# A fused decoder layer: sums for the up-projection made by adding DMAs inside the mixing layer

## The chip, the cores and the metric

The kernel runs on one core of a Trainium2 chip. The metric is the device time of one execution in microseconds (us); the kernel before takes 1341.85 us (median of three runs, 1340.24 to 1342.94).

Five engines work beside each other, each through its own list of instructions in order: PE (TensorE, matmuls), DVE (VectorE), ACT (ScalarE), POOL (GpSimd) and SP (SyncE, which here only issues transfers). DMAs are issued from SP, from ACT and from POOL; those of POOL can add to what lies at the destination instead of replacing it, and only they do so here. An instruction that waits holds up whatever stands behind it on its engine, and a DMA that waits holds up the later DMAs of the same issuing engine.

## The reference

One decoder layer in float32, on 1024 tokens of width 1024: a norm, one wide input projection, two attention mixers (differential and sliding-window), gates, an output matrix, a residual sum, a second norm, and a gated feed-forward part with a causal convolution. What this change touches begins at the output matrix:

```python
        merged = jax.nn.sigmoid(g_da) * (y_da @ w_br_da[l]) + jax.nn.sigmoid(g_sw) * (y_sw @ w_br_sw[l])
        x = x + merged @ w_mix_out[l]
        xn = rmsnorm(x, norm_ffn_w[l])
        x = x + conv_ffn(xn, w_up[l], conv_w[l], conv_b[l], w_down[l])
    return rmsnorm(x, norm_final_w)
```

`conv_ffn` multiplies by `w_up` (1024 x 5632), runs a convolution of width 3 along the tokens, multiplies one half by the silu of the other, and multiplies by `w_down` (2816 x 1024).

## The kernel before, in words

Everything is kept transposed: features on the 128 partitions, the 1024 tokens along the free axis, in two halves of 512 (`H2`). A feature block is called m or k.

**Two parts per operand.** Each float32 operand is split into a high part (a cast to float32r on ACT) and a low part (the difference, on DVE), and each product is three matmuls: high by high, high by low, low by high (`mm3`, `product`). A weight unit is therefore a load (SP), a cast on ACT (`wh`, line 142, or `sh`/`wh`, line 121) and a subtraction on DVE (`wl`, line 144, or `sl`/`wl`, line 123). The raw weights of all stages turn through three buffers called `raw` (`RAW = 3`), each free again when its subtraction is done.

**Seven products in place of eight.** The input projection, the output matrix ("mixing layer"), the up-projection ("hidden layer") and the down-projection each use a Strassen-Winograd scheme: a 2 x 2 block product by seven block products P1 to P7 (`STAGES`), whose operands include sums: S1 to S4 of weight blocks, T1 to T4 of activation blocks.

**Where sums are made before.** For the mixing layer and the down-projection the weight sums are made far ahead in DRAM by `sums_of` (line 85): copies issued by SP and adding DMAs issued by POOL, `md` for the mixing layer, four of its 32 steps behind each of the nine weight pairs of the input projection. For a pair of weight blocks of the input projection and of the up-projection they are made on POOL by `sum_pair` (four operations, lines 107 to 110), from two loads (`raw`, line 102, and `rv`, line 104); `split_pair` then splits A11/A12, S1/S2, S3/S4 and A22.

**The mixing layer** (`mix`, line 853) has seven stages of two halves each. This document calls these fourteen halves units 0 to 13: P1 is units 0 and 1, P2 units 2 and 3, P5 4 and 5, P6 6 and 7, P3 8 and 9, P7 10 and 11, P4 12 and 13. A unit takes one weight load of 512 KB and runs 24 matmuls (two feature blocks, four k, three matmuls each) into PSUM banks; behind each 12 of them DVE adds the bank to the residual tile `xm` (line 955, "eviction"). Four of the seven stages finish a quarter of the new x: P2 (blocks 0 to 3, first half of the tokens), P3 (0 to 3, second half), P7 (4 to 7, second half) and P4 (4 to 7, first half). `finish` (line 888) then stores it to DRAM (`x2d`, issued by ACT), squares it on ACT and adds the square to `rstd` on POOL (line 898). `onward` (line 900), at most one block later, makes the operands of the hidden layer from it: x times the norm weight, and the sums and splits B11, T1, B22, T3, T2, T4 and B21.

- For blocks 0 to 3, ACT multiplies `xm` by the norm weight in place (line 904), so it has to wait until the store of that same tile is done.
- The sums are DVE operations: `t` (line 908), `u` (line 913), `t + u` (line 914) and T4's `u` (line 919), four of each, 128 x 512.
- In P3, behind unit 9's weights, `sum_pair` loads the first up-projection pair into two of the three `raw` buffers and sums it on POOL. It is split only at the end of `mix` (`split_pair`, lines 121 and 123), so both buffers are held until then.

**The hidden layer** (`hidden`, line 993) runs 22 pairs of 84 matmuls each, pair 0 in the order P1, P5, P3, P7, P2, P6, P4 with the norm's column sums in between. After each pair DVE recombines the seven banks (`recombine`, line 469), POOL or DVE scales by `rstd`, ACT and DVE run the convolution (lines 1153 to 1156).

**What sets the order.** A scheduler orders each engine's list by priorities (`tc.high_priority` moves work forward) and by hand-written rules (`tc.issue_after` keeps work behind a named instruction). Tile pools free memory for later pools.

## Time and profile before

| what | value |
|---|---|
| median of three runs | 1341.85 us (1340.24 to 1342.94) |
| the profiled execution | 1340.74 us, span of the trace 1339.0 us |
| busy share of the span | PE 98%, PE weight loads 81%, DVE 81%, ACT 47%, POOL 38% |
| granted TensorE clock | 0.990 of full speed on average |
| packets' time on the DMA queues | SP's 40.8%, POOL's 8.5%, ACT's 3.6% of 16 engines' span |
| mixing layer in the trace | 587.7 to 690.7 us |
| hidden layer in the trace | 690.7 to 1118 us |

How to read the rows: in the table by stretches of time each row gives the start and end in us from the span's start, the length, then for each engine its busy us and in brackets its instructions, then the granted TensorE clock, the busy share of the 16 DMA engines and GB/s. In lists in order of time, the first column is the start in us and the second the busy us of the (merged) entry; a bracket at the end gives the idle time before it and what ended it. "SPq" and the like are instructions that only the engine's queue handles, such as issuing a DMA. Grouped rows give min/median/max in ns, then first and last start. A matmul row gives 0.39 us for one matmul, but they are pipelined: the distance from one start to the next is what counts.

### The profile page before, as it was taken

To read this page: it belongs to the slowest core of one execution; us is meant where nothing else is said; L and a number is where in the kernel's file an instruction comes from. 1 tells how busy PE (TensorE), PEld (TensorE's weight loads), DVE (VectorE), ACT (ScalarE), POOL (GpSimd) and SP (SyncE) were. 2 spreads that over 40 slices of the span, in tenths; PEclk is the share of its full clock that TensorE was granted. 3 is DMA by queue.
4 is the path that set the end of the run, shared out by engine and by line. 5 is a ranking of instruction groups with operands and counts; after the bars stand their busy time and mean duration, and the time that the engine had idled before them with its cause. 6 is when DMAs were issued, how large, how long until landed. Compare 5 with 4: busy or idle time off the path is not lost.

```text
span 1339.0 us, 17280 instructions
## 1 busy us (share of the span) xinstructions
PE 1306.0 (98%) x6162; PEld 1084.2 (81%) x6162; DVE 1087.8 (81%) x1518; ACT 634.4 (47%) x1002; POOL 510.3 (38%) x396
## 2 busy tenths in 40 slices
PE   9999999999999999998889999999999999999997
PEld 7888888888888878886668888888888887888886
DVE  8856685388898977656887999999999999896855
ACT  9432232376667774334554334343343335554543
POOL 0448662010101017742435666676667642000002
PEclk9999999999999999999989999999999999999999
DMA  7346665966554146567342434663636237953534
GB/s 290 134 178 160 227 214 149 281 169 177 157 135 150 64 160 187 165 215 201 110 142 91 181 127 134 168 202 105 202 122 160 80 103 249 331 183 119 162 96 146
DMA packets 81414, 221.71 MB, mean 166 GB/s; under 512 B 9008, under 2 KB 16816, under 8 KB 81072
## 3 DMA queue, kind: packets, MB, share of 16 engines
q1 hardware_dynamic: 61536, 183.37, 40.8%
q0 software_dynamic: 6912, 19.93, 8.5%
q10 hardware_dynamic: 12880, 17.31, 3.6%
q8 instruction: 48, 0.79, 0.2%
q14 instruction: 38, 0.31, 0.1%
HBM read 167.62 MB, written 80.22 MB: 185 GB/s over the span
## 4 chain that ended last, share of the span: by engine, by line
PE 76%; DVE 11%; issue 5%; DMA 3%; ACT 2%; POOL 2%; SPq 0%; POOLq 0%; DVEq 0%; ACTq 0%
PE t L990 29%; PE y L1209 9%; PE d L1209 7%; PE g L163 4%; PE g L164 4%; PE g L165 4%; PE m L953 3%; PE sc L649 3%; DVE c L1155 2%; DVE wl L123 2%; PE t L665 1%; DMA rv<-in_w_up 1%; PE sc L165 1%; PE sc L164 1%; PE sc L163 1%
## 5 line engine op out<-in xcount | busy, mean ns | idle before, releaser
L144 DVE TENSOR_TENSOR wl<-raw,wh 128x1024 fp32r<-128x1024 f32 (+2 forms) x91 | 111.6, 1229 | 47.2 <-ACT wh L142 37.5
L142 ACT CAST wh<-raw 128x1024 fp32r<-128x1024 f32 (+2 forms) x91 | 80.3, 885 | 85.8 <-PE y L1209 44.1
L1139 POOL TENSOR_TENSOR us<-us,rstd 128x1024 f32<-128x1024 f32 x42 | 94.9, 2307 | 47.6 <-DVE us L482 31.2
L1153 ACT ACTIVATE c<-us,vecs 128x1024 f32<-128x1024 f32 x44 | 54.8, 1247 | 116.0 <-POOL us L1139 110.5
L990 PE MATMUL t<-T,sh 128*128 128x512 f32 x352 | 109.2, 391 | 0.2 <-DVE u L477 0.2
L180 POOL TENSOR_TENSOR rs<-ms,mhalf 128x8 f32<-128x8 f32 (+2 forms) x9 | 14.2, 1580 | 238.8 <-DVE ms L178 232.6
L123 DVE TENSOR_TENSOR sl<-sf,sh 128x1024 fp32r<-128x1024 f32 x62 | 90.6, 1462 | 14.8 <-ACT sh L121 14.7
L121 ACT CAST sh<-sf 128x1024 fp32r<-128x1024 f32 x62 | 64.6, 1044 | 79.9 <-PE t L990 40.6
L107 POOL TENSOR_TENSOR sf<-rv 128x512 f32<-128x512 f32 x30 | 56.8, 1894 | 105.2 <-DMA rv<-in_w_up 52.9
L990 PE MATMUL t<-x,wh 128*128 128x512 f32 x248 | 82.2, 389 | 0.0
L953 PE MATMUL m<-x,wh 128*128 128x512 f32 x192 | 63.6, 418 | 15.1 <-ACT wh L142 15.1
L990 PEld LDWEIGHTS t<-T,sh 128*128 128x128 f32 x352 | 65.5, 188 | 15.0 <-DVE u L477 1.6
L163 PE MATMUL g<-xh,wh 128*128 128x512 f32 x176 | 70.9, 403 | 1.5 <-ACT g L578 1.5
L1156 DVE SCALAR_TENSOR_TENSOR c<-us,vecs,c 128x1024 f32<-128x1024 f32 x44 | 72.2, 1674 | 0.1
L164 PE MATMUL g<-x,wh 128*128 128x512 f32 x176 | 70.3, 400 | 0.0
L165 PE MATMUL g<-xh,wl 128*128 128x512 f32 x176 | 70.2, 399 | 0.0
L1155 DVE SCALAR_TENSOR_TENSOR c<-us,vecs,c 128x1024 f32<-128x1024 f32 x44 | 67.4, 1561 | 1.9 <-ACT c L1153 1.7
L990 PE MATMUL t<-T,sl 128*128 128x512 f32 x176 | 68.6, 390 | 0.0
L990 PE MATMUL t<-x,sh 128*128 128x512 f32 x212 | 68.2, 389 | 0.0
L109 POOL TENSOR_TENSOR sf<-raw,rv 128x512 f32<-128x512 f32 x30 | 54.0, 1798 | 35.5 <-DVE sl L123 35.5
L123 DVE TENSOR_TENSOR wl<-raw,wh 128x1024 fp32r<-128x1024 f32 (+1 forms) x32 | 65.9, 2059 | 0.1
L1209 PE MATMUL y<-h,wh 128*128 128x512 f32 (+1 forms) x224 | 65.2, 375 | 0.0
(335 smaller groups left out, 3944.0 us busy)
## 6 DMA issues: line engine op xcount, KB each, us to landing
u<-qd SPq DMA_DIRECT2D x72, 256.0 KB, 6.4
raw<-in_w_up SPq DMA_DIRECT2D x23, 512.0 KB, 4.8
raw<-in_w_in SPq DMA_DIRECT2D x22, 512.0 KB, 4.9
hd<-c SPq DMA_DIRECT2D x22, 512.0 KB, 2.6
sdP<-in_w_down POOLq DMA_DIRECT2D x16, 704.0 KB, 8.3
rv<-in_w_up SPq DMA_DIRECT2D x21, 512.0 KB, 3.6
hc<-hd SPq DMA_DIRECT2D x33, 256.0 KB, 5.5
gr<-gd SPq DMA_DIRECT2D x16, 512.0 KB, 4.6
```

The costliest lines, as they stand in the source:

```text
L123: low = nc.vector.tensor_tensor(lo, src, hi.bitcast(F32), ALU.subtract)
L142: self.hi = nc.scalar.copy(wh, raw)
L144: self.lo = (eng or nc.vector).tensor_tensor(wl, raw, wh.bitcast(F32), ALU.subtract)
L163: nc.tensor.matmul(ps, wh[:, kc + o, :], ah, start=first and n == 0, stop=False)
L164: nc.tensor.matmul(ps, wh[:, kc + o, :], al, start=False, stop=False)
L165: nc.tensor.matmul(ps, wl[:, kc + o, :], ah, start=False, stop=last and n == len(kcs) - 1)
L953: nc.tensor.matmul(ps, v[:, m % 2 * 4 + k, :], x, start=start and k == i == 0, stop=k == 3 and i == 2, skip_group_check=True)
L990: nc.tensor.matmul(ps, (ah, ah, al)[p][:, k, :], (bh, bl, bh)[p], start=first and n == p == 0, stop=last and p == 2 and n == len(ks) - 1, ...
L1139: i = (nc.vector if m % NF == 0 else nc.gpsimd).tensor_tensor(us[:, 2:], us[:, 2:], self.rstd, ALU.mult)
L1155: nc.vector.scalar_tensor_tensor(c, us[:, 1:T + 1], cw[1], c, ALU.mult, ALU.add)
L1156: nc.vector.scalar_tensor_tensor(c, us[:, 0:T], cw[0], c, ALU.mult, ALU.add)
L1209: nc.tensor.matmul(ps, v[:, k - k0, :], x, start=start and k == i == 0, stop=k == HK - 1 and i == 2, skip_group_check=True)
```

## The change: what it does

**Weight sums of the first two up-projection pairs** (`NPRE = 2`) are made in DRAM, in new tensors `ud`, by `sums_up`: for each of the two pairs four copies issued by SP and four adding DMAs issued by POOL, 256 KB each, in a chain (S1 and S3 from copies of weights, S2 from S1, S4 from S2). They follow the mixing layer's sums in one chained list, and the loop of the input projection now issues six steps behind each weight pair instead of four. As a DMA only adds, S2, S3 and S4 come out in forms whose signs are turned; activation operands take the signs over, and `recombine` adds or subtracts accordingly (`pre`), and gives its operands in the other order.

**Loads of these two pairs** go by `part_pair`: four parts, each one load through `raw`, one cast on ACT, one subtraction on DVE: A11/A12, S1/S2, S3/S4, and A22 (half the size). POOL's four operations per pair go away for both. In `mix`, parts 1 and 2 of pair 0 are asked for behind the weights of units 12 and 13, and parts 0 and 3 after the last unit. `sum_pair` in P3 goes away.

**Activation sums** are made by 16 adding DMAs, each 256 KB within SBUF, issued by POOL: `onward` and its 16 DVE sums go away. ACT makes a scaled copy (8 more ACT operations, for B22 and B21), and the work is put off by whole units: a function `later` files it under a unit number, and `run_due` issues it behind that unit's weight cast and subtraction. Scaling in place comes two units after the eviction, T1 is split one unit after its add; B22 is split one unit after the eviction, T3 two and T2 three; B21 one, T4 two. What falls due after unit 13 is issued at the end of `mix`.

**Order and memory.** `next_w` in `mix` stands under `tc.high_priority(60)`; the splits of the merged activations stand at the start of the next stage, behind its weights. The pool `sfp` of POOL's sums is opened only in `hidden`, after the `xm` tiles are given up.

```diff
@@ ahead
             if nk == "pair":
                 first, skip = eng or (False, 0)
-                self.wq.append(self.split_pair(*self.sum_pair(src, first), skip))
+                if len(src) == 3:
+                    w = {}
+                    for part in range(4):
+                        w.update(self.part_pair(src, part))
+                    self.wq.append(w)
+                else:
+                    self.wq.append(self.split_pair(*self.sum_pair(src, first), skip))
...
+    def sums_up(self):
+        nc, d = self.nc, self.ud
+        row = lambda j, r: self.w_up[j].rearrange("p k c -> p (k c)")[:, r * H2:(r + 1) * H2]
+        copy = lambda n, src: lambda j: nc.sync.dma_start(d[j][:, n], src(j))
+        add = lambda n, o, r: lambda j: nc.gpsimd.dma_start(d[j][:, n], row(j + o, r), accum_op=ALU.add)
+        for step in (copy(0, lambda j: row(j + NF, 0)), copy(2, lambda j: row(j + NF, 0)), add(0, NF, 1), add(2, 0, 0),
+                     copy(1, lambda j: d[j][:, 0]), add(1, 0, 0), copy(3, lambda j: d[j][:, 1]), add(3, 0, 1)):
+            for j in range(NPRE):
+                step(j)
+                yield
+
+    def part_pair(self, src, part):
+        nc = self.nc
+        raw = self.tl(self.wp, [P, 1 if part == 3 else 2, 4, P], "raw", bufs=RAW)
+        nc.sync.dma_start(raw.rearrange("p a k c -> p (a k) c"), (src[0], src[2][:, 0:2].rearrange("p a (k c) -> p (a k) c", k=4),
+                          src[2][:, 2:4].rearrange("p a (k c) -> p (a k) c", k=4), src[1][:, 4:8])[part])
+        n = (("A11", "A12"), ("S1", "S2"), ("S3", "S4"), ("A22",))[part]
+        pool, h, l = (self.uw, "sh", "sl") if part in (1, 2) else (self.wp, "wh", "wl")
+        hi = self.tl(pool, [P, len(n), 4, P], h, F32R)
+        self.hi = nc.scalar.copy(hi, raw)
+        lo = self.tl(pool, [P, len(n), 4, P], l, F32R)
+        self.lo = nc.vector.tensor_tensor(lo, raw, hi.bitcast(F32), ALU.subtract)
+        if part == 0:
+            self.front = self.hi.ins, self.lo.ins
+        return {name: (hi[:, i], lo[:, i]) for i, name in enumerate(n)}
@@ project
-            sums = self.sums_of(self.md, self.w_mix, H2)
+            sums = chain(self.sums_of(self.md, self.w_mix, H2), self.sums_up())
...
-                for _ in range(4):
+                for _ in range(6):
@@ recombine
-        tt(c11, ps["P2"], s1, ALU.add)
-        tt(u2, ps["P6"], s1, ALU.add)
-        tt(u3, ps["P7"], u2, ALU.add)
...
+        sub = lambda flag: ALU.subtract if flag else ALU.add
+        tt(c11, s1, ps["P2"], sub(o))
+        tt(u2, ps["P6"], s1, sub(pre))
+        tt(u3, u2, ps["P7"], sub(pre))
...
@@ mix
-        def onward(m, hf):
...
-                if hf == 0:
-                    self.B["B11", k] = parts(up["B11", k], x)
-                else:
-                    tt(t, x, col(k, 0), ALU.subtract)
-                    self.B["T1", k] = parts(up["T1", k], t)
-            elif hf:
-                self.B["B22", k] = parts(up["B22", k], x, wcol(m))
-                u = col(k, 1)
-                stt(u, x, wcol(m), u, ALU.mult, ALU.subtract)
-                tt(t, u, col(k, 0), ALU.add)
...
+        add = lambda x, y: nc.gpsimd.dma_start(x, y, accum_op=ALU.add)
+        later = lambda i, f: due.setdefault(i, []).append(f)
...
+            if m < 4 and hf == 0:
+                later(i + 2, lambda: (nc.scalar.mul(x, x, wcol(m)), put("B11", k, x)))
+            elif m < 4:
+                later(i + 2, lambda: (nc.scalar.mul(x, x, nw[:, m:m + 1]), add(col(k, 0), x)))
+                later(i + 3, lambda: put("T1", k, col(k, 0)))
             elif hf:
+                t = x22[k // 2][:, k % 2]
+                later(i + 1, lambda: (nc.scalar.mul(t, x, wcol(m)), put("B22", k, t), add(col(k, 1), t)))
+                later(i + 2, lambda: (add(col(k, 0), t), put("T3", k, col(k, 1))))
+                later(i + 3, lambda: put("T2", k, col(k, 0)))
             else:
+                t = col(m, 1)
+                later(i + 1, lambda: (nc.scalar.mul(t, x, nw[:, m:m + 1]), put("B21", k, t), add(col(k, 0), t)))
+                later(i + 2, lambda: put("T4", k, col(k, 0)))
...
+        def run_due(i):
+            with tc.issue_after(self.hi.ins), tc.issue_after(self.lo.ins):
+                for f in due.pop(i, ()):
+                    f()
...
                 for h in range(2):
-                    w = self.next_w()
+                    with tc.high_priority(60):
+                        w = self.next_w()
+                        if stage == "P4":
+                            self.uw = uw
+                            w0.update(self.part_pair(pair, 1 + h))
+                            self.uw = None
...
-                    if stage == "P3" and h:
-                        i = [e[1] for e in self.wsrc].index("pair")
-                        pair = self.sum_pair(self.wsrc.pop(i)[0], True)
+                    run_due(i)
...
-        with tc.high_priority(100):
-            return self.split_pair(*pair)
+        with tc.high_priority(60):
+            for part in (0, 3):
+                w0.update(self.part_pair(pair, part))
+        run_due(i)
+        run_due(i + 1)
+        run_due(i + 2)
...
+        return w0
```

More of the change, by code (lines that the diff above doesn't have):

```diff
@@ L2 @@
 from contextlib import ExitStack, nullcontext
+from itertools import chain
 import numpy as np
@@ L27 @@
 RAW = 3
+NPRE = 2
 HP, HPB, HR = 7, 13, 11
@@ L216, in run @@
             self.md = {n: self.dp.tile([4, P, H2], F32, name="md" + n) for n in ("P5", "P6", "P3", "P7")}
+            self.ud = [self.dp.tile([P, 4, H2], F32, name=f"ud{j}") for j in range(NPRE)]
             self.sd = {n: self.dp.tile([4, P, HK * P], F32, name="sd" + n) for n in ("P5", "P6", "P3", "P7")}
@@ L258, in plan @@
                 src.append((w, KC))
-        src += [((self.w_up[j], self.w_up[j + NF]), "pair") for j in range(NF)]
+        src += [((self.w_up[j], self.w_up[j + NF], *self.ud[j:j + 1]), "pair") for j in range(NF)]
         for name in STAGES:
@@ L863, in mix @@
         self.B = {}
[L864 to L865 removed]
+        self.tctx, sctx = ExitStack(), ExitStack()
         xmp = self.tctx.enter_context(tc.tile_pool(name="xmp", bufs=1, reuse_waits="tile"))
[L867 to L873 removed]
+        xm = {m: xmp.tile([P, T], F32, name=f"xm{m}") for m in range(KC)}
+        sqp = sctx.enter_context(tc.tile_pool(name="sqp", bufs=1, reuse_waits="tile"))
+        sqs = [sqp.tile([P, 2, H2], F32, name="sqs")]
+        x22 = [self.tl(self.cpl, [P, 2, H2], "c") for _ in range(2)]
+        nw = self.st.tile([P, KC], F32, name="nw")
+        nc.vector.tensor_scalar(nw, self.vecs[:, C_NF:C_NF + KC], -1.0, None, ALU.mult)
+        acc, nsq = self.rstd, []
         col = lambda m, hf: xm[m][:, hf * H2:(hf + 1) * H2]
         wcol = lambda m: self.vecs[:, C_NF + m:C_NF + m + 1]
+        due = {}
         def parts(t, src, scale=None):
@@ L886, in parts, with put, finish @@
             return hi, lo
-        def finish(m, hf):
-            x = col(m, hf)
+        def put(name, k, src, scale=None):
+            t = self.slot(k) if name == "T3" else self.slot(4 + k) if name == "B21" else up[name, k]
+            self.B[name, k] = parts(t, src, scale)
+        add = lambda x, y: nc.gpsimd.dma_start(x, y, accum_op=ALU.add)
+        later = lambda i, f: due.setdefault(i, []).append(f)
+        def finish(i, m, hf):
+            x, k = col(m, hf), m % 4
             nc.scalar.dma_start(self.x2d[m, :, hf * H2:(hf + 1) * H2], x)
@@ L951, in mix @@
                             hi, lo = M[b, k]
-                            for i, (v, x) in enumerate(((w[0], hi), (w[0], lo), (w[1], hi))):
-                                nc.tensor.matmul(ps, v[:, m % 2 * 4 + k, :], x, start=start and k == i == 0, stop=k == 3 and i == 2, skip_group_check=True)
+                            for j, (v, x) in enumerate(((w[0], hi), (w[0], lo), (w[1], hi))):
+                                nc.tensor.matmul(ps, v[:, m % 2 * 4 + k, :], x, start=start and k == j == 0, stop=k == 3 and j == 2, skip_group_check=True)
                         x = col(m + o, hf)
```

78 lines of the change are left out of this document (32 added, 46 removed).

## The prediction

> **What bounds the kernel now.** I read the page first (busy shares and slices), then the table by stretches, then PE's own order in time, and last ACT, DVE, POOL and SP beside PE's gaps.
>
> ```profile
> span 1339.0 us, 17280 instructions
> PE 1306.0 (98%) x6162; PEld 1084.2 (81%) x6162; DVE 1087.8 (81%) x1518; ACT 634.4 (47%) x1002; POOL 510.3 (38%) x396
> ```
> ```profile
> 60.00:238.00 178.00, 178.00 (x787) 147.40 (x786) 116.89 (x121) 50.69 (x60) 101.93 (x68) 1.00 0.62 192
> 609.60:624.50 14.90, 9.06 (x31) 6.27 (x31) 10.03 (x14) 10.80 (x17) 6.56 (x6) 0.89 0.70 191
> 624.50:652.50 28.00, 28.00 (x124) 23.19 (x125) 21.41 (x25) 13.21 (x20) 6.73 (x5) 1.00 0.52 156
> 652.50:690.90 38.40, 26.04 (x89) 19.31 (x88) 38.24 (x45) 21.93 (x34) 18.24 (x10) 0.78 0.39 130
> 720.00:1118.00 398.00, 397.42 (x1750) 327.63 (x1748) 390.05 (x339) 159.54 (x175) 249.22 (x175) 1.00 0.46 142
> ```
> ```profile
> 63.99 171.36 PE t L990 x756
> ```
>
> PE is busy 1306 of 1339 us, so only its gaps can be won. 756 matmuls in 171.36 us give its pace, 0.2267 us each. The mixing layer needs 336 of them, 76.2 us, and takes 103.1 (587.66 to 690.74). The loss sits in two stretches: 14.90 − 31 × 0.2267 = 7.9 us, and 38.40 − 89 × 0.2267 = 18.2 us. Their granted clock is 0.89 and 0.78: after a wait PE also runs slow.
>
> ```profile
> 612.99 0.84 PE L953 MATMUL m<-x,wh 128*128 128x512 f32 x2 [3.41 <-ACT wh L142]
> 621.81 1.70 PE L953 MATMUL m<-x,wh 128*128 128x512 f32 x6 [1.04 <-ACT wh L142]
> 667.72 2.07 PE L953 MATMUL m<-x,wh 128*128 128x512 f32 x4 [5.14 <-ACT wh L142]
> 680.79 2.08 PE L953 MATMUL m<-x,wh 128*128 128x512 f32 x4 [5.47 <-ACT wh L142]
> 684.44 1.05 PE L953 MATMUL m<-x,wh 128*128 128x512 f32 x2
> 711.59 0.61 PE L990 MATMUL t<-B,wh 128*128 128x512 f32 x2
> ```
> ```profile
> 611.28 0.72 ACT L904 ACTIVATE xm<-xm,vecs 128x512 f32<-128x512 f32 x1 [5.38 <-DMA x2d<-xm]
> 611.91 1.03 ACT L142 CAST wh<-raw 128x1024 fp32r<-128x1024 f32 x1
> 660.60 0.71 ACT L884 ACTIVATE B<-xm,vecs 128x512 fp32r<-128x512 f32 x1
> 661.21 1.12 ACT L881 CAST T<-c 128x512 fp32r<-128x512 f32 x2
> 676.76 1.99 ACT L121 CAST sh<-sf 128x1024 fp32r<-128x1024 f32 x2 [1.61 <-DVE x L882]
> ```
> ```profile
> SPq L132 <- DVE wl L144: 52.4, 9, 9.7
> ```
>
> Every large wait is for a weight cast on ACT, for two reasons. In the first stretch ACT stood 5.38 us at the in-place scaling, which waited for the store of its tile, with the cast behind it. In the second, DVE is full (38.24 of 38.40), and two of three raw buffers are held by the up-projection pair, so SP waits for DVE's subtractions before it can load (52.4 us in all).
>
> **The change, part by part.** I time it against the pace: unit n starts at 587.66 + 5.44 n, so unit 10 at 642.1, unit 13 at 658.4, the end at 663.8.
>
> *First stretch.* Scaling moves two units (10.9 us) behind the eviction; the store took 7.30 us (the chain of waits), so ACT no longer stands. What is late next: unit 6's cast. The stores land by 611 to 613, then six ACT operations of about 0.6 us and the cast of 1.0 end at 618, against the need at 620.3. Return 7.9; 0.5 kept back for that margin.
>
> ```profile
> 603.90 7.30 DMA x2d<-xm
> ```
> ```profile
> L908 DVE TENSOR_TENSOR c<-xm x4: 677/934/1782, 648.7 to 660.0; 128x512 f32<-128x512 f32 x4
> L913 DVE SCALAR_TENSOR_TENSOR xm<-xm,vecs,xm x4: 737/741/1069, 657.8 to 672.0; 128x512 f32<-128x512 f32 x4
> L914 DVE TENSOR_TENSOR c<-xm x4: 676/678/679, 659.4 to 676.6; 128x512 f32<-128x512 f32 x4
> L919 DVE SCALAR_TENSOR_TENSOR xm<-xm,vecs,c x4: 743/1419/1828, 684.9 to 695.7; 128x512 f32<-128x512 f32 x4
> L898 POOL TENSOR_TENSOR rstd<-rstd,t x14: 1287/1624/3772, 607.1 to 695.7; 128x512 f32<-128x512 f32 x14
> ```
>
> *Second stretch.* Sixteen DVE sums go: 4 × (0.93 + 0.74 + 0.68 + 1.42) = 15.1 us. The raw buffers turn freely, so unit weights arrive two units ahead, and pair 0's parts take their turns: S1/S2 and S3/S4 when the subtractions of units 11 and 12 are done (645 and 650), A11/A12 behind unit 13's (656), landed by 661. Return 18.2 while the adds land in time.
>
> *The adds.* Sixteen issues on POOL, each followed by a landing that ACT and DVE wait for.
>
> ```profile
> L851 POOL DMA_DIRECT2D mr<-mr x16: 852/876/1052, 517.0 to 623.7; - x16
> DMA to landing us min/median/max: 3.2/7.0/9.7
> ```
> ```profile
> mr<-mr POOLq DMA_DIRECT2D x1, 256.0 KB, 3.2
> mr<-mr POOLq DMA_DIRECT2D x1, 256.0 KB, 5.1
> ```
>
> Asked for one by one, the same kind of add took 3.2 us alone (issued 616.9, 620.1 and 622.5), 5.1 close behind another (623.7), and 9.7 under the loads of x (601.3). The new adds come in twos, where the DMA share was 0.39; I take 5.1, and 3.2 and 9.7 as ends. An issue costs POOL 0.88 and holds nothing else but the square sums. ACT's new list, with the eight operations it gains, has five places where it waits for adds or PE waits behind them:
> (1) T1: ACT scales block 1 by 644.7; POOL, behind a square sum (1.6), issues at 645.7; landed 650.8. Then a copy (0.56), four scalings (0.63 each, by the starts 660.60 and 661.21) and unit 13's cast (1.0) end at 655, needed 658.4. Hidden by 3.4.
> (2) Hand-over: after the eviction in unit 12 (657.8) ACT has, ahead of A11's cast, a store issue (0.4), two pair casts (1.99), seven operations of 0.56, two scalings (1.3); with the cast (1.0) it ends at 666.3. The adds it waits for land by 660. PE is done at 663.8: **2.5 us wait**, new.
> (3) T3, blocks 2 and 3: issued 663 to 664, landed 669, used by PE at 675.
> (4) T4, blocks 0 and 1: landed 676; the casts of B21 blocks 2 and 3 stand behind and end at 679; PE's need is 666.3 + 8.2 + 1.0 + 4.1 = 679.6. Hidden, with nothing to spare.
> (5) T4, blocks 2 and 3: landed 683, needed about 687.
>
> *Slow clock after (2).* A 3.41 us wait was followed by 1.75 us of loss within its unit (620.6 − 612.99 − 0.42 − 5.44); the 1.04 us wait by 0.2. For 2.5 I take 1.0. [...]
>
> *VectorE beside POOL.* Where POOL computes, a DVE operation of 0.68 grows up to 1.78. Fifteen square sums stay, eight sums of pairs go. At most 10 × 0.6 = 6 us on DVE's list, of which its gaps (25 us of work in 28) take more than half: 2.0 charged, 0 and 6 as ends.
>
> *Input projection.* Sixteen more DMAs, six steps behind each pair.
>
> ```profile
> 183.99 0.33 SPq L104 DMA_DIRECT2D rv<-in_w_in  x1
> 200.18 1.73 POOL L110 TENSOR_TENSOR sf<-raw,sf 128x512 f32<-128x512 f32 x1
> 214.40 2.40 POOL L465 TENSOR_TENSOR us<-us,rstd 128x1024 f32<-128x1024 f32 x1 [6.81 <-DVE us L482]
> 232.43 0.32 SPq L608 DMA_DIRECT2D f<-qd  x1
> mdP<-in_w_mix POOLq DMA_DIRECT2D x16, 256.0 KB, 6.6
> mdP<-mdP SPq DMA_DIRECT2D x8, 256.0 KB, 8.8
> ```
>
> In SP's list the last pair's second load now stands behind a copy that waits for an add issued just before (6.6): 184 becomes 190, and the pair's sums end by 206 in place of 202. PE reaches that pair at 63.99 + 8 × 19.04 = 216. At the end the chain copy, add, copy (8.8 + 6.6 + 8.8) holds POOL's L465 from 214.4 to about 220, and with it the stores on SP ahead of the attention's first load at 232.4. Cost 0; without cover every us of these would be PE's; ends 0 and 3.
>
> ```profile
> 718.91 0.67 DVE L483 TENSOR_TENSOR us<-u,t 128x512 f32<-128x512 f32 x1
> 719.50 0.68 DVE L482 TENSOR_TENSOR us<-t,u 128x512 f32<-128x512 f32 x1
> ```
>
> *Recombination* with its operands turned costs the same (0.67 and 0.68). *Pair 1* has no POOL sums; its last part and pair 2's load wait for a raw buffer until about 684, so pair 2's sums end near 695, as far behind the start of pair 1 as before: 0.
>
> **Sum.** −7.9 − 18.2 + 0.5 + 2.5 + 1.0 + 2.0 = −20.1: pair 1 starts near 691.5 in place of 711.59, and from there the hidden layer runs as before. Against the profiled execution (1340.74; span 1339.0) that is 1320.6; the median shown is 1.1 higher, so 1341.85 − 20.1 = 1321.8, given as **1322**. Ends: all 26.9 won, 1315, a little less if POOL's eight sums also free DVE: 1314. Within 0.2% (2.7 us) is about what a measurement cannot tell from no change.
>
> **Rivals.**
> *A: the adds land like the slowest seen, 9.7 us.* Places (2) to (5) then add up: A11's cast at 673.3, B21 at 695, T4 at 705, pair 1 at 708: 3.6 won, 1338. For it: adds and weight loads share the 16 DMA engines. Against it: the 0.70 stretch had three at 3.2. [...]
> *B: VectorE sets the pace of the hidden layer.*
>
> ```profile
> 704.60 0.69 DVE L476 TENSOR_TENSOR us<-t,s 128x512 f32<-128x512 f32 x1 [5.68 <-PE t L990]
> 713.94 1.34 DVE L123 TENSOR_TENSOR sl<-sf,sh 128x1024 fp32r<-128x1024 f32 x1 [4.18 <-ACT sh L121]
> ```
>
> It is busy 390.05 of 398 us there, and had idled 5.68 and 4.18 us around pair 0. If it cannot do without these 9.9 us, 10.2 of the 20.1 stay: 1331.6. Against it: it idled because PE and the pair's sums were not there yet, and both come as much earlier.
> *C, slower: the same five waits with landings over 10.6 us*, the point where the gain is gone (3.6 us left at 9.7, about 4 us lost per us of landing). At 12 us: 1346. Only the sixteen adds queuing on one queue speak for it.
> *D: the change only moves the wait* from the units to the hand-over: what is due behind unit 13 all meets there. 18 back of 20: 1340. Against it: ACT's list there is 8.5 us long, not 20.
>
> **How the numbers follow.** Forecast (15 to 27 won) 0.60, A 0.13, B 0.11, C 0.11, D 0.05. Faster than by 0.2%: 0.60 + 0.13 + 0.11 − 0.01 = 0.83; the same 0.05; slower 0.12. The range runs from 1314 to A's 1338 and leaves out C, D and a little of A, 0.18.
>
> **What would show it.** Right: no wait for unit weights over 1 us in the mixing layer, its matmuls ended near 664 to 666, one wait of 2 to 4 us at the first up-projection matmul, adds of `xm` landing in 4 to 6 us, PE still full from 60 to 238. Wrong: ACT standing long at casts that read `xm` behind a DMA; waits of PE inside pair 0 at B21 or T4; SP late in the projection; or a hidden layer with new waits for DVE.

## The result, and the profile after

The changed kernel takes 1350.48 us (1349.57 to 1351.85) against 1342.0 (1340.24 to 1342.94) for the kernel before, runs beside each other on one chip: a ratio of 1.0066 with a 95% interval of 1.0048 to 1.0083. It is slower by about 9 us, where a gain of 20 was forecast. The profiled execution took 1351.85 us.

The head of the page of the changed kernel, span and busy shares:

```profile
span 1350.1 us, 17338 instructions
PE 1324.8 (98%) x6162; PEld 1088.5 (81%) x6162; DVE 1036.6 (77%) x1503; ACT 639.0 (47%) x1010; POOL 512.1 (38%) x412
```

PE has the same 6162 instructions as before and is busy 18.8 us longer (1306.0 to 1324.8). VectorE is busy 51 us less. So what the change meant to take away is gone, and something that it does not touch takes longer. The table by stretches of the changed kernel (columns as before) says where:

```profile
60.00:238.00 178.00, 178.00 (x767) 144.34 (x766) 105.64 (x113) 48.14 (x58) 107.36 (x71) 1.00 0.71 203
593.92:682.47 88.55, 80.08 (x338) 64.19 (x336) 62.69 (x81) 49.30 (x76) 31.40 (x31) 0.95 0.83 231
682.47:720.00 37.53, 33.64 (x131) 27.51 (x132) 28.35 (x31) 18.79 (x30) 21.29 (x20) 0.83 0.77 219
720.00:1118.00 398.00, 398.00 (x1729) 324.08 (x1728) 365.52 (x336) 160.22 (x171) 241.29 (x172) 1.00 0.44 136
```

From 60 to 238 PE was full before and is full after, at a granted clock of 1.00 both times, but 767 matmuls go through where 787 did. From 720 to 1118 it is 1729 in place of 1750, without an idle moment. The chain of waits of the changed kernel shows the same 756 matmuls of the projection, and the long run of the hidden layer:

```profile
65.04 175.68 PE t L1043 x756
...
657.27 7.31 DMA xm<-xm
...
689.52 9.72 DMA xm<-xm
...
702.48 3.20 PE t L207 x16
...
720.31 401.17 PE t L1043 x1740
```

756 matmuls take 175.68 us: 0.2324 us each where the prediction's pace was 0.2267 (171.36 us). The waits of PE in the changed kernel (in all, times, longest), the three longest:

```profile
PE t L1043 <- ACT wh L126: 6.7, 1, 6.7
PE t L1043 <- ACT x L919: 3.9, 1, 3.9
PE m L1014 <- DVE gr L861: 1.8, 1, 1.8
```

None of them is for a unit weight of the mixing layer; those (15.1 and 3.1 us before) are gone. The two at L1043 are new, both in the first up-projection pair. The 16 adding DMAs of `xm`, with their time from issue to landing:

```profile
L930 POOL DMA_DIRECT2D xm<-xm x8: 877/988/1206, 655.4 to 701.6; - x8
L930 POOL DMA_DIRECT2D xm<-c x8: 862/876/1349, 667.6 to 685.4; - x8
DMA to landing us min/median/max: 3.4/6.8/9.7
```

And ScalarE's list around the two waits of PE (which ended at 682.47 and 701.68):

```profile
675.04 0.62 ACT L919 CAST x<-xm 128x512 fp32r<-128x512 f32 x1
678.07 0.62 ACT L919 CAST x<-xm 128x512 fp32r<-128x512 f32 x1 [2.41 <-DMA xm<-c]
...
681.39 1.55 ACT L126 CAST wh<-raw 128x1024 fp32r<-128x1024 f32 x2
...
696.68 0.62 ACT L919 CAST T<-xm 128x512 fp32r<-128x512 f32 x1 [2.77 <-DMA xm<-xm]
699.26 0.62 ACT L919 CAST T<-xm 128x512 fp32r<-128x512 f32 x1 [1.97 <-DMA xm<-xm]
...
701.02 1.12 ACT L919 CAST x<-xm 128x512 fp32r<-128x512 f32 x2
```

The cast of A11 (681.39) stands behind a T3 cast that waited 2.41 us for a landing, and B21's last casts (701.02) stand behind two T4 casts that waited 2.77 and 1.97 us. Earlier, at 661.75 and 664.61, two T1 casts began after waits of 1.83 and 1.70 us for their adds. The landing of 7.31 us in the chain of waits above is that of one of these adds; unit 13's cast and the list up to the hand-over stand behind it.

By section, from the starts of PE's first matmuls in each (right128 is explained below; it is the changed kernel with its matmuls back at the old pace):

| section of the span, us | before | changed | right128 |
|---|---|---|---|
| to the mixing layer | 587.7 | 593.9 | 588.6 |
| mixing layer to the first matmul of pair 0 | 103.1 | 88.6 | 83.0 |
| pair 0 to the hidden layer's unbroken run | 27.3 | 37.8 | 37.6 |
| that run, 1740 matmuls | 395.3 | 401.2 | 394.4 |
| the rest | 225.6 | 228.6 | 223.7 |
| span | 1339.0 | 1350.1 | 1327.2 |

### The profile page after: what moved, and what is told of

Read it like the earlier page. It is cut to its first block, busy times and chain, and to the rows that moved or that the text cites. A ratio compares the mean times of both kernels' runs of the same rounds, so it can differ in the third digit from the quotient of the medians.

```text
span 1350.1 us, 17338 instructions
## 1 busy us (share of the span) xinstructions
PE 1324.8 (98%) x6162; PEld 1088.5 (81%) x6162; DVE 1036.6 (77%) x1503; ACT 639.0 (47%) x1010; POOL 512.1 (38%) x412
## 4 chain that ended last, share of the span: by engine, by line
PE 87%; POOL 4%; DMA 3%; DVE 2%; issue 2%; ACT 1%; SPq 0%; POOLq 0%; ACTq 0%; DVEq 0%
PE t L1043 44%; PE y L1263 9%; PE d L1263 7%; PE m L1014 4%; PE g L199 3%; PE g L200 3%; PE g L201 3%; PE sc L687 3%; POOL mr L869 2%; DMA gr<-gd 2%; POOL gr L845 2%; DMA xm<-xm 1%; PE t L703 1%; PE t L806 1%; PE sc L775 1%
## 5 line engine op out<-in xcount | busy, mean ns | idle before, releaser
L180 DVE TENSOR_TENSOR wl<-raw,wh 128x1024 fp32r<-128x1024 f32 (+2 forms) x91 | 100.0, 1100 | 70.9 <-ACT wh L178 58.2
L157 ACT CAST sh<-sf 128x1024 fp32r<-128x1024 f32 x58 | 60.6, 1050 | 113.8 <-PE t L1043 99.5
L1043 PE MATMUL t<-T,sh 128*128 128x512 f32 x352 | 111.2, 397 | 0.0
L143 POOL TENSOR_TENSOR sf<-rv 128x512 f32<-128x512 f32 x29 | 53.3, 1837 | 110.2 <-DMA rv<-in_w_up 45.5
L1043 PE MATMUL t<-x,wh 128*128 128x512 f32 x248 | 84.8, 399 | 3.9 <-ACT x L919 3.9
L159 DVE TENSOR_TENSOR sl<-sf,sh 128x1024 fp32r<-128x1024 f32 x58 | 77.9, 1344 | 9.1 <-ACT sh L157 9.1
L1043 PEld LDWEIGHTS t<-T,sh 128*128 128x128 f32 x352 | 66.6, 190 | 15.4
L1210 DVE SCALAR_TENSOR_TENSOR c<-us,vecs,c 128x1024 f32<-128x1024 f32 x44 | 70.3, 1630 | 0.1
L1043 PE MATMUL t<-T,sl 128*128 128x512 f32 x176 | 69.3, 394 | 0.0
L1043 PE MATMUL t<-x,sh 128*128 128x512 f32 x212 | 68.4, 390 | 0.0
L1209 DVE SCALAR_TENSOR_TENSOR c<-us,vecs,c 128x1024 f32<-128x1024 f32 x44 | 66.0, 1537 | 1.2 <-ACT c L1207 1.2
L691 DVE CUSTOM_DVE_ANT_0 L<-sc,bias 128x128 f32<-128x128 f32 (+7 forms) x64 | 47.7, 752 | 17.0 <-PE sc L687 14.2
L670 POOL MEMSET aT<- 128x128 f32 x32 | 6.2, 205 | 142.9 <-PE t L716 102.0
```

Of the source, the lines that this page charges most:

```text
L159: low = nc.vector.tensor_tensor(lo, src, hi.bitcast(F32), ALU.subtract)
L180: self.lo = (eng or nc.vector).tensor_tensor(wl, raw, wh.bitcast(F32), ALU.subtract)
L1043: nc.tensor.matmul(ps, (ah, ah, al)[p][:, k, :], (bh, bl, bh)[p], start=first and n == p == 0, stop=last and p == 2 and n == len(ks) - 1, ...
L1209: nc.vector.scalar_tensor_tensor(c, us[:, 1:T + 1], cw[1], c, ALU.mult, ALU.add)
L1210: nc.vector.scalar_tensor_tensor(c, us[:, 0:T], cw[0], c, ALU.mult, ALU.add)
```

## The experiments

**Where a slower matmul could come from.** A clue lies in which matmuls are slower. The groups by form of the kernel before, three of the hidden layer's (busy us, then mean ns of one):

```profile
L990 PE MATMUL t<-x,wh 128*128 128x512 f32 x248 | 82.2, 389 | 0.0
...
L990 PE MATMUL t<-x,sh 128*128 128x512 f32 x212 | 68.2, 389 | 0.0
...
L990 PE MATMUL t<-B,sh 128*128 128x512 f32 x176 | 54.2, 389 | 0.0
```

The same groups of the changed kernel:

```profile
L1043 PE MATMUL t<-x,wh 128*128 128x512 f32 x248 | 84.8, 399 | 3.9 <-ACT x L919 3.9
...
L1043 PE MATMUL t<-x,sh 128*128 128x512 f32 x212 | 68.4, 390 | 0.0
...
L1043 PE MATMUL t<-B,sh 128*128 128x512 f32 x176 | 55.1, 394 | 0.0
```

The moving operand `x` is slower by 10 ns with the weights `wh` and by 1 ns with `sh`. Part of the 10 lies behind the waits, where the granted clock was 0.83 (682.47 to 720): from 725 to 1100 us, at 1.00, the means are 394 and 389. For the moving operand `B` it is the other way round: 394 with `sh`, and in the same 375 us 391 with `wh`. What differs is memory. The small new tile `nw` of the change (the negated norm weights, 8 numbers per partition) is taken from the pool `st`, which keeps four buffers of it: 4 x 32 bytes. Every pool behind `st` on SBUF's left side moves up by those 128 bytes; the pools that grow from the right side stay. Start of some pools in bytes, from the two compiled programs:

```
pool            before   changed   modulo 256
wp  (wh, wl)      9216      9344     0 -> 128
xc  (B11,T1,B22) 46080     46208     0 -> 128
ar  (x slots)   196096    196096     0 -> 0
uw  (sh, sl)    130560    130560     0 -> 0
```

`wh`, `wl` and `B` thus lie on the left side, `sh`, `sl` and the `x` slots on the right: the pairs that are 5 ns slower take their operands from different sides. *Theory P*, a guess from this table: a matmul is slower where its weights and its moving operand start at different offsets modulo 256 bytes. *Theory T*: addresses do not matter; the time goes to what the change issues.

**left128**: the kernel before, nothing changed but the padding ahead of the left side.

```diff
-LPAD, RPAD = 480, 480
+LPAD, RPAD = 608, 480
```

> The kernel before, with only the pad at the left end of the on-chip memory 128 bytes longer, so that every tile of the left side (weights among them) moves by 128 bytes and the right side stays. Theory P (a matmul's pace depends on whether its weights and its moving operand lie at the same offset modulo 256 bytes): start to start goes from 0.2267 to about 0.232 us in the input projection (756 matmuls in about 175.7 us in place of 171.4), about 24 us in all: 1366 us (1358 to 1374). Theory T (the adding DMAs and their traffic slow TensorE): none is added here, 1342 us and 171.4.

1358.47 us (1358.05 to 1358.84), ratio 1.0121 (1.0106 to 1.0136): 128 bytes of padding alone cost 16.4 us, at the low end of theory P's range (24 us were expected). In its chain of waits the projection's matmuls take exactly what they take in the changed kernel:

```profile
65.39 175.68 PE t L990 x756
```

**left256**: the same by 256 bytes (`LPAD = 736`).

> The kernel before with the left pad 256 bytes longer. Theory P: the offsets modulo 256 are as before, so 1342 us within 3 us and the 756 matmuls in 171.4 us. If any shift whatever slowed the matmuls: about 1366 us.

1341.8 us (1339.92 to 1344.7), ratio 1.0003 (0.9992 to 1.0013), and 171.36 us for the 756 matmuls. Moving the left side by 256 bytes costs this kernel nothing that shows.

**right128**: the changed kernel, with the right side moved by the same 128 bytes as `nw` moves the left.

```diff
-LPAD, RPAD = 480, 480
+LPAD, RPAD = 480, 608
```

> The changed kernel with the pad at the right end 128 bytes longer, so that both sides lie at 128 modulo 256. Theory P (what counts is the offset of the two operands against each other): pace 0.2267 us, 1326 us (1320 to 1332), as with the small tile moved. If the absolute address counts (multiples of 256 are fast): pace 0.232 or more everywhere, 1350 us or above. Theory T: 1350 us.

1330.22 us (1328.98 to 1332.28), ratio to the kernel before 0.9912 (0.9897 to 0.9927). So in this kernel the pace follows the offset of one operand against the other, not where they lie: with both sides at 128 modulo 256 the old pace is back. Its chain of waits, with the unbroken runs of the mixing and hidden layers:

```profile
588.71 54.41 PE m L1014 x240
...
709.10 394.43 PE t L1043 x1740
```

240 in 54.41 and 1740 in 394.43 us are 0.2267 each. Theory T falls: the same change, with the same transfers, is 20.3 us faster for 128 bytes of padding.

**nw_in_xmp**: the changed kernel with `nw` taken from another pool, so that the operands of the matmuls have their old offsets again.

```diff
-        nw = self.st.tile([P, KC], F32, name="nw")
+        nw = xmp.tile([P, KC], F32, name="nw")
```

> The changed kernel with one edit: the small tile of negated norm weights lies in the pool of the residual tiles and no longer in the pool of small tiles, so that the pools behind the latter return to the addresses of the kernel before. Theory P: the pace returns to 0.2267 us and the time falls by about 24 us, to 1326 us (1320 to 1332): the gain of the mixing layer comes out. Theory T: 1350 us, pace 0.232.

1335.23 us (1333.14 to 1337.9), ratio 0.9949 (0.9932 to 0.9966): the second way to the old pace (394.43 us for the 1740) agrees in direction, but it is 5 us above right128 and outside P's range. Its mixing layer starts 4 us later than right128's (592.45 and 588.71); the projection's sums, below, cost differently from build to build.

**left64, left32**: the kernel before with the left side moved by 64 and by 32 bytes (`LPAD = 544` and `512`).

> The kernel before with every pool of the left side moved by 64 bytes, the right side as it was. Nothing else differs. Theory P (weights and moving operand at different offsets modulo 256 bytes slow each matmul from 0.227 to 0.2325 us): 1358 like the move by 128, or a pace between the two. Rival (only an offset of 128 does it): 1342.

> The kernel before with the left side moved by 32 bytes. If any offset between weights and moving operand modulo 256 (or 64) bytes slows the matmuls, 1358 to 1361 as with 64 and 128 bytes and 171.4 us for the 756 matmuls of the projection becomes about 176; if only multiples of 64 do, 1342.

1359.9 us (1358.52 to 1361.43), ratio 1.0128 (1.0108 to 1.0148), and 1362.19 (1360.25 to 1362.42), ratio 1.014 (1.0126 to 1.0155). Both need 176.40 us for the 756 matmuls, where the move by 128 took 175.68 and that by 256 the 171.36 of the kernel before.

| projection | before | left32 | left64 | left128 | left256 | changed | right128 |
|---|---|---|---|---|---|---|---|
| matmuls from 66 to 230 us, PE full in all | 726 | 705 | 704 | 708 | 725 | 707 | 725 |

**What the two new waits are.** With the pace out of the way right128 is the kernel that the prediction described, and it gains 11.8 us by its span where 20.1 were forecast. Its waits of PE:

```profile
PE t L1043 <- ACT wh L126: 6.7, 1, 6.7
PE t L1043 <- ACT x L919: 4.2, 1, 4.2
```

*Theory H*: each wait is a matter of the order of ScalarE's list and can be taken out by itself. *Theory F*: they have one cause behind them, what the pair's operands wait for, and a wait taken out comes back one product later. Three edits of right128:

**b21_first**: T4 is split one unit later, so that B21's scaled copies stand ahead of T4's casts.

```diff
-                later(i + 2, lambda: put("T4", k, col(k, 0)))
+                later(i + 3, lambda: put("T4", k, col(k, 0)))
```

> The changed kernel with both sides of SBUF moved alike (right128), and one edit more: T4 is split one unit later, so that on ScalarE the scaled copies for B21, blocks 2 and 3, stand ahead of T4's casts of blocks 0 and 1. Theory H (the second wait of right128, 4.2 us at B21, is only ScalarE's list: it stands at T4's cast, which waits 8 to 9 us for an adding DMA, with B21 behind it): the 4.2 us go, and so does the slow clock behind them (16 column sums in 3.27 us where the kernel before has 1.71, and about 8 matmuls at 0.43 instead of 0.227): 4.2 + 1.6 + 1.6 = 7.4 us less than right128's 1330.2, 1323 (1320 to 1326). Theory F (adds and loads share a full set of DMA engines, or VectorE is full, so PE only waits one product later, at T4): 1328 to 1331, with a wait at L1043 for T.

1329.49 us (1326.76 to 1331.79), ratio 0.9899 (0.9874 to 0.9925): theory F's value. The wait for B21 is gone, but 1.5 us are now waited for T on ScalarE and 1.4 for splits on VectorE, and the first wait is 7.4.

**front0**: part 0 (A11, A12) is asked for in unit 13 and part 2 (S3, S4) after the last unit.

```diff
-                            w0.update(self.part_pair(pair, 1 + h))
+                            w0.update(self.part_pair(pair, 1 - h))
...
-            for part in (0, 3):
+            for part in (2, 3):
```

> right128, with part 0 of the first pair (A11, A12) asked for in unit 13 and part 2 (S3, S4) after the last unit, the other way round than in the changed kernel; T4 as in the changed kernel. The wait of 6.7 us at the first up-projection matmul goes in both theories, and with it about 3 us of slow clock (14 matmuls at 0.427 instead of 0.227). Theory H+F (the adds of T4 are asked for when units 12 and 13 are done, not when the pair starts, and B21 stands behind them): the second wait grows by nearly as much, 4.2 to 11 or more, and the time stays at 1327 to 1331. Rival (the two waits are independent of each other, and each is worth its own length): 1330.2 - 9.7 = 1320.5 (1318 to 1324).

1335.13 us (1332.42 to 1336.3), ratio 0.9936 (0.9916 to 0.9957). The first wait is gone and nothing is won: the time lies above the expected 1331 even, though its mixing layer also starts 4.3 us later than right128's (592.82 and 588.55). The waits of PE in front0:

```profile
PE t L1043 <- ACT x L919: 7.2, 1, 7.2
PE t L1043 <- DVE sl L128: 3.3, 1, 3.3
```

**front0_b21**: both edits.

> Both edits, that of b21_first and that of front0. Theory H: both waits go, 1330.2 - 9.7 - 7.4 = 1313 (1310 to 1318), which is the best that the prediction thought possible. Theory F: the adds' landing of 7 to 10 us on full DMA engines then ends last; a wait at T4 or B21 of 5 us or more stays, 1320 to 1330.

1328.89 us (1327.64 to 1330.4), ratio 0.9897 (0.9881 to 0.9913), not the 1313 of theory H: no long wait is left, but five of 1.0 to 1.9 us, and the hidden layer's unbroken run starts at 709.24, where right128's starts at 709.10. As the start of the mixing layer varies too, count from there: to the unbroken run it takes 120.6 us in right128, 118.6 in b21_first, 123.4 in front0 and 118.3 in front0_b21. Both edits together return 2 us. Theory H falls; of theory F the time came true and its sign, a wait of 5 us or more, did not. front0_b21 is the fastest complete kernel here all the same, by 13 us against the kernel before and 22 against the changed one (medians; the changed kernel was not measured beside it).

**What stands behind them.** In front0_b21 two things are full at once behind unit 12:

```profile
667.50:691.00 23.50, 16.08 (x60) 11.12 (x59) 22.35 (x22) 15.84 (x28) 15.91 (x15) 0.95 1.04 270
```

VectorE is busy 22.35 of 23.5 us, and the packets fill the 16 DMA engines (share 1.04; before, it was 0.39 in the second stretch). Theory V (VectorE, stretched by POOL's work beside it, sets pair 0) and theory L (the landing of the adding DMAs does) name one each. Two kernels each take one away.

**no_sq**: front0_b21 without POOL's sums of squares of blocks 4 to 7, beside which VectorE's splits grow longer (two T splits take 4.18 us).

```diff
-                nc.gpsimd.tensor_tensor(a, a, sq, ALU.add)
+                if m < 4:
+                    nc.gpsimd.tensor_tensor(a, a, sq, ALU.add)
```

> front0_b21 with POOL's ten... eight sums of squares of blocks 4 to 7 (L943) left out, so the norm is computed from half of its terms. Behind unit 12 VectorE is full in front0_b21 (22.4 of 23.5 us from 667.5 to 691), and five of its groups run longer beside these sums: the split of T at 668.02 takes 4.18 us for two (1.28 alone), the next 2.33, 2.85, 4.32, 2.36; about 9 us more than alone. Theory V (VectorE stretched by POOL sets pair 0): first pair 41.6 us becomes 33 to 36, the time 1328.9 - 6 to 9 = 1320 to 1323. Theory L (the landing of the adding DMAs on full DMA engines sets it): 1326 to 1330.

1330.12 us (1328.91 to 1332.22), ratio 0.9906 (0.9889 to 0.9924): nothing won, so theory V alone does not explain it. VectorE does get its time back: the two T splits that took 4.18 us in front0_b21 take 1.28. But PE waits 6.7 us for B21, behind an add that took 10.51 us to land. The landing of no_sq's 16 adds (in front0_b21 the median is 8.0, the slowest 9.6):

```profile
DMA to landing us min/median/max: 3.4/7.7/12.0
```

**no_adds**: front0_b21 without the twelve adding DMAs for T3, T2 and T4.

```diff
-                later(i + 1, lambda: (nc.scalar.mul(t, x, wcol(m)), put("B22", k, t), add(col(k, 1), t)))
-                later(i + 2, lambda: (add(col(k, 0), t), put("T3", k, col(k, 1))))
+                later(i + 1, lambda: (nc.scalar.mul(t, x, wcol(m)), put("B22", k, t)))
+                later(i + 2, lambda: put("T3", k, col(k, 1)))
...
-                later(i + 1, lambda: (nc.scalar.mul(t, x, nw[:, m:m + 1]), put("B21", k, t), add(col(k, 0), t)))
+                later(i + 1, lambda: (nc.scalar.mul(t, x, nw[:, m:m + 1]), put("B21", k, t)))
```

> front0_b21 with the twelve adding DMAs for T3, T2 and T4 left out, so these operands miss a term and nothing waits for a landing. ScalarE's waits for landings (2.65, 0.62, 0.71, 2.62, 0.97 and 0.69 us from 667 to 692) go, and 12 of the transfers that fill the DMA engines. Theory L: pair 0 falls by 8 to 14 us, 1315 to 1321. Theory V: the sums of squares still stretch VectorE's splits and it stays the last, 1324 to 1329.

1323.85 us (1320.66 to 1324.25), ratio 0.9853 (0.9834 to 0.9871): 5.0 us less than front0_b21: a gain, as theory L had it, but only half of the 8 to 14 us that it asked for. The unbroken run starts 5.5 us earlier, although the mixing layer did not start earlier:

```profile
591.57 54.41 PE m L1014 x240
...
703.75 394.43 PE t L1043 x1740
```

Pair 0, from its first matmul to that run, takes 27.3 us before, 41.6 in front0_b21 and 36.2 in no_adds: these twelve adds, with their landing and their share of the transfers, hold 5.4 of the 14.3 us lost. In no_adds it is VectorE that ends last: PE's waits of pair 0 are for its splits (1.9 us in three, 0.7 in one), and its operations make up 17.7 of the 23.8 us of the chain of waits from 660.15 to 683.96, such as

```profile
677.49 4.61 DVE x L920 x4
```

Four such splits would take 2.6 us, by the 1.28 that two of them take in front0_b21 (at 672.13). So two limits lie close behind each other: with the adds in place, relieving VectorE wins nothing, and without these adds VectorE sets pair 0. What taking away both would return was not run; the four adds for T1, one of which takes 6.31 us in no_adds' chain of waits, are in all of these kernels.

**The first stretch alone. before_defer**: the kernel before, with the scaling in place put off by two units.

```diff
-        acc, nsq, late = self.rstd, [], []
+        acc, nsq, late, c = self.rstd, [], [], 0
...
-                            late.append((m + o, hf))
-                        while len(late) > (m < 3 and o == 0):
-                            onward(*late.pop(0))
+                            late.append((c, m + o, hf))
+                        while late and late[0][0] + (4 if stage in ("P2", "P5") else m < 3 and o == 0) <= c:
+                            onward(*late.pop(0)[1:])
+                        c += 1
```

> The kernel before with one part of the change alone: the scaling in place of blocks 0 to 3, first half (L904), comes two units (four blocks) later, everything else as before. The prediction's first term gives -7.9 + 0.5 = -7.4: 1334.6 (1332 to 1337), the waits of 3.41 and 1.04 us at unit weights gone. Rival (what is won in units 4 and 5 only makes the later units run into VectorE and the raw buffers earlier, and the second stretch grows by it): 1339 to 1343.

1337.46 us (1336.43 to 1337.95), ratio 0.996 (0.9944 to 0.9975): 4.7 us, between the two expectations. Its waits of PE in the mixing layer:

```profile
PE m L953 <- ACT wh L142: 10.9, 3, 5.1
PE m L953 <- DVE wl L144: 4.2, 4, 1.5
```

They were 15.1 and 3.1 us, longest 5.5. The 3.41 is gone, and VectorE's part grows by 1.1: a piece of what the first stretch returns is taken again in the second.

**The sums in the projection. before_ud**: the kernel before with the sixteen DMAs of `sums_up`, six steps behind each pair, whose result nothing reads.

```diff
+            self.ud = [self.dp.tile([P, 4, H2], F32, name=f"ud{j}") for j in range(NPRE)]
...
-            sums = self.sums_of(self.md, self.w_mix, H2)
+            sums = chain(self.sums_of(self.md, self.w_mix, H2), self.sums_up())
...
-                for _ in range(4):
+                for _ in range(6):
```

> The kernel before, with the sums of the two up-projection pairs made in DRAM by the same sixteen DMAs, six steps behind each pair of the input projection, and never read. The prediction charged the projection 0 with 0 and 3 as ends: 1342 (1341 to 1345). Rival (the chain of copies and adds delays the projection's own loads, as the later start of the mixing layer in the aligned builds suggests, 588.7 to 593 in place of 587.7): 1345 to 1347.

1345.57 us (1341.55 to 1349.21, ten runs), ratio 1.0024 (1.0011 to 1.0037): 3.2 us by the ratio, and a wider spread than any other kernel here. POOL's list in before_ud shows what the prediction had in mind, an add that waits for a copy ahead of the projection's last scaling (L480 here):

```profile
220.63 0.83 POOL L104 DMA_DIRECT2D ud<-in_w_up  x1 [7.34 <-DMA ud<-ud]
225.37 0.82 POOL L104 DMA_DIRECT2D ud<-in_w_up  x1 [3.91 <-DMA raw<-in_w_in]
225.92 2.70 POOL L480 TENSOR_TENSOR us<-us,rstd 128x1024 f32<-128x1024 f32 x1
```

The scaling starts at 225.92 where it started at 214.40, and in this execution PE then stood 1.7 us in the attention.

**before_ud8, front0_b218**: before_ud and front0_b21 with eight steps behind each pair, so that the chain ends behind the sixth of the nine pairs, two pairs earlier.

```diff
-                for _ in range(6):
+                for _ in range(8):
```

> before_ud with eight steps of the sums behind each weight pair instead of six, so that all 48 are out behind the sixth pair of nine. Theory Q (POOL stood 7.34 us at an add that waited for a copy, ahead of the last scaling of the projection, which began at 225.92 instead of 214.40 and delayed the stores and first loads of the attention): 1342 to 1343, no wait of PE near 254. Rival R (what costs is that sixteen more transfers share the DMA engines, wherever they stand): 1344 to 1347.

> front0_b21 with eight steps behind each pair. Theory Q: 1328.9 - 3 = 1326 (1324.5 to 1327.5), the mixing layer starting near 588 instead of 591. Rival R: 1328 to 1331.

1351.71 us (1349.89 to 1353.06), ratio 1.0065 (1.0052 to 1.0078), and 1335.28 (1333.48 to 1335.89), ratio 0.9942 (0.993 to 0.9955): both are slower by 6 us than with six steps, worse than either theory said. The wait of PE moves into the projection itself:

```profile
PE t L1005 <- DVE wl L137: 4.7, 2, 3.9
```

In before_ud8 PE is busy 171.63 of the 178 us from 60 to 238, with six steps 177.69, so most of the 9 us is lost there. SP waits 11.6 us in all, up to 7.7 at a time, at copies of `ud` that wait for an add; with six steps it is 15.9 us and also up to 7.7. The sum of these waits therefore does not tell the two apart. That the place matters, because weight loads of pairs still to come stand behind the chain, is argued and not shown, and whether the extra traffic has a share was not told apart.

## Why the prediction was wrong, point by point

The forecast was 1322 us, the time 1350.5.

- **The step that failed is the pace.** "I time it against the pace", 0.2267 us a matmul, and "from there the hidden layer runs as before": that the matmuls of the changed kernel cost what they cost before was assumed and never examined. In the changed kernel those of the projection take 0.2324. Against right128 this is 20.3 us by the medians, spread over the whole kernel: between the two profiled executions 22.9, by the table of sections 5.3 to the mixing layer (4.3 of it in the 756 matmuls above), 5.6 in it (1.8 of that as a wait for an operand of the merged activations), 0.2 in pair 0, 6.8 in the hidden layer's run, 4.9 in the rest. The rest of the 5.3 can be the projection's sums, which vary. No rival had it, and the working passed over the one line that causes it, the tile `nw`, since it costs no time as an operation.
- **First and second stretch, −7.9 and −18.2: right together.** Without the offset the mixing layer from its first matmul to that of pair 0 takes 83.0 us, 6.7 of them the wait at its end: its 336 matmuls run through in 76.3, where the pace asks for 76.2. All but 0.1 of the 26.9 us is back. Alone, the first stretch returned 4.7 and not 7.4 (before_defer): the two terms are not independent, as a part of the first's return is lost again in the second stretch.
- **Hand-over (2), +2.5 and 1.0 of slow clock: right in place, too small.** 6.7 us in the changed kernel and in right128. "The adds it waits for land by 660" failed: a T3 cast ahead of A11's waited 2.41 us for a landing. So did place (1), T1, "Hidden by 3.4": ScalarE stood 1.83 and 1.70 us at its casts (2.33 and 0.61 in right128), and the chain of waits runs through that landing. Slow clock: granted 0.79 over the 13.53 us behind the wait in the changed kernel's trace, 2.8 us.

```profile
682.47:696.00 13.53, 13.53 (x47) 10.85 (x48) 12.92 (x12) 7.71 (x14) 9.27 (x8) 0.79 1.07 269
```

- **T4 and B21 (4), "hidden, with nothing to spare": wrong.** 3.9 us of wait in the changed kernel, 4.2 in right128, and behind it a granted clock of 0.50 (701.68 to 705.70 in the changed kernel): the 16 column sums there take 3.20 us in the changed kernel's chain of waits above, and 1.68 in that of the kernel before:

```profile
704.51 1.68 PE t L171 x16
```

  Pair 0 in all takes 10.2 us more than before in right128.
- **The adds' landing, taken at 5.1: a mis-sized term behind both.** Median 6.8, slowest 9.7, the upper end given; the DMA share in the row above is 1.07, where the prediction read 0.39 off a kernel that was not yet loading ahead. From 657 to 700 us SP's queue moves 5.19 MB (3.67 before) beside ACT's 2.10 of stores, as before, and 3.67 of the adds; that the loads start there because the raw buffers are freed was not shown. Adds and loads on the same 16 DMA engines are rival A's mechanism, and here half of its price: A takes 16.5 us off the gain of 20.1, and right128 misses 8.3. The sixteen issues took 0.86 to 1.35 us each, near the 0.88 charged. That landing is all of the loss is not shown: no_adds returns 5.0 us.
- **VectorE beside POOL, +2.0: seen in the operations, hidden in the time.** Two T splits take 4.18 us beside the sums of squares (front0_b21) and 1.28 without them (no_sq), but no_sq, which takes half of those sums away, wins nothing while the slowest add lands later still (12.0 us). In no_adds VectorE is the limit.
- **Rival B (VectorE paces the hidden layer): no.** With the pace restored the run of 1740 takes 394.4 us against 395.3, and VectorE does less there.
- **Projection, 0 with ends 0 and 3: the mechanism was named, the size not taken.** 3.2 us done alone, 0.9 in right128, more in other builds.
- **Rival D (the wait only moves to the hand-over): in part.** Of the 26.9 us won in the units, 17.0 are lost again at the hand-over and in pair 0 (6.8 and 10.2); front0 and front0_b21 show that moving one wait mostly moves it further.

Two of the prediction's own signs of being wrong appeared, ScalarE standing at casts behind a DMA and a wait of PE inside pair 0 at B21. For the pace it had none: its sign of being right, PE full from 60 to 238, held while 20 matmuls fewer went through.

The terms as right128 has them: −26.9 + 6.8 + 10.2 + 0.9 (to the mixing layer) − 0.9 − 1.9 (hidden layer's run and the rest) = −11.8, the difference of the spans. The remainder to the changed kernel, 22.9, is the offset but for the two open parts named above: the wait of 1.8 and what the projection's sums vary by.

## What to carry to other kernels

A tile of a few bytes is part of a change (here `nw` moved the left side by 128 bytes, and undoing that was worth 20.3 us): compare the pool addresses of the two programs before taking a pace over, and when PE is busy longer with the same number of matmuls and a full clock, look there first. The adds landed at a median of 6.8 us and not at 5.1 where the DMA share was 1.07 and not 0.39: take the landing time of a DMA from the traffic there will be, not from that of the stretch as it was. The waits at the head of the pair whose operands are made late moved along when the list was reordered: that returned 2 us at most, where leaving out twelve late adds returned 5. And a kernel that leaves one suspect out, and wins nothing, clears it only as long as the other suspect is still there.

## What the runs showed of the hardware

In this kernel the start-to-start time of the matmuls (128x128 weights, 128x512 moving operand, float32r) changed with how weights and moving operand lie against each other in SBUF: the 756 of the projection took 171.36 us at equal offsets modulo 256 bytes (before, left256), 175.68 at a difference of 128 (left128, changed), 176.40 at 64 and at 32 (left64, left32), all at a granted clock of 1.00. That is 2.5 to 2.9% of a matmul; over this kernel 16.4 to 19.5 us. Moving both sides by 128 (right128) gave the old pace back, 0.2267 us each. Within the changed kernel, from 725 to 1100 us, `x` with `wh` and `B` with `sh`, which lie at different offsets, took 394 ns, `B` with `wh` 391 and `x` with `sh` 389. Why is open: no trace shows what a matmul waits for inside. Only differences of 32, 64, 128 and 256 bytes were tried, and always by moving a whole side, so a rule that says 256 is taken from these four alone.
